# Turning the written key of an RWKV-7 chunk recurrence: PE transposes and ScalarE copies, or a DRAM round trip and VectorE

## The chip, the cores and the metric

The kernel runs on one core of a Trainium2 chip. The metric is device time in microseconds (us) of one execution. The times shown are of three runs; one further execution is profiled.

## What is computed

One layer of a hybrid trunk: batch 1, 512 positions, width 2048, everything in float32. Half of the width is an RWKV-7 group of 16 heads of 64 with a generalized delta rule, the other half a pooling group. In short form:

```
h = rms_norm(x, norm_g);  z = h @ w_in            # columns: r, k, v, two low-rank inputs, gate | pool input, pool gate
zs = zs + (token_shift(zs) - zs) * mu                # r, k, v and the low-rank inputs
w = exp(-exp(-softplus(-(w0 + tanh(wd) @ w_up)) - 0.5));  a = sigmoid(a0 + ad @ a_up)
kk = normalize(k * k_k);  k = k * (1 + (a - 1) * k_a)      # per head of 64
for each t:                                          # 16 heads, state S is 64x64
    S = S * w[t] - (S @ kk[t]) (a[t] * kk[t])^T + v[t] k[t]^T
    y[t] = S @ r[t]
y = head_group_norm(y) + (sum(r * k * r_k)) * v
pool = multiscale means of the pool input - itself, a 256x256 map per group, a scale
x = x + concat(y * silu(gate), pool * silu(pool gate)) @ w_out
x = x + sigmoid(x @ w_pg + b_pg) * (p @ w_ple);  out = rms_norm(x, final_g)
```

## The kernel before

**Work and staging.** The 16 heads are taken as 8 head pairs j of 128 channels, the 512 positions as 8 chunks of 64. A float32 product is split in three matmuls on rounded halves (`mm3`): each weight chunk is loaded as `raw_*` by SP, rounded by ScalarE into `whi_*`, and the rest `wlo_*` is left by VectorE. There are four `raw`, four `whi` and four `wlo` buffers, so a `raw` load waits for the `wlo` that read its buffer last. The names carry the stream and the chunk: `raw_r` chunk 2 belongs to the projection r of the next pair.

**Order.** TensorE (PE) runs in the order in which the program is written (`keep_in_program_order`). Its long projections are a stream of fill matmuls, and `pump(n)` puts n units of that stream between dependent steps of the recurrence. The other engines get their order from a scheduler when the kernel is built; each then runs its list in order. SP issues nearly all DMAs, and stands still while one of them waits.

**One head pair.** `prepare(j)` scales the streams. `bk` (128 channels x 8 chunks x 128) holds the written keys k and the removed keys kk, channels on the partitions. `scores(j)` multiplies `bk` with `ar` into the masked chunk matrices `mt`. Four `nd` DMAs take their 32x32 triangles to DRAM, two `n` DMAs bring them back spread over all partitions. `invert(j)` solves all triangles at once by 31 substitution steps on VectorE (`tm`, then `xw`), stores `xw` as `xd` and loads the inverse `x1`. For pair 0 the steps run without a recurrence beside them; for pair j+1 they are dealt out inside the recurrence of pair j, each after that chunk's leading VectorE instruction (`issue_after`, HS and HN in `step`). `gather(j)` transposes v into `uv` and `bk` into `bkn` (positions on the partitions), lets PE fill, transposes the diagonal block of `x1` on VectorE (`y`), and builds the rest of the inverse with PE (`pq`) and the products `mv`. `norm_key` and `scale_key` (the RECIPROCAL) belong to the pair after.

**Recurrence.** `recur(j)` does per chunk: PE `py` (state times `ar`), VectorE `zs`, PE `pu` (inverse times `zs`), ScalarE copies into `uv`, PE `ps` (`bkn` of the chunk times `uv`), VectorE `sbd`, the next state. The fill between them is HC = 6, 9 and 9 units. Before chunk 1 the scores of pair j+1 are computed (`between`).

Of the kernel before, what the change touches and what calls it, by code (L numbers as in the profile page):

```python
# [9 lines left out]
F32 = mybir.dt.float32  # L10
# [5 lines left out]
P = 128  # L16
T = 512
# [4 lines left out]
NJ = DR // P  # L22
LORA = 64
C = 64
NCH = T // C
# [9 lines left out]
def trunk_kernel(ctx: ExitStack, tc: tile.TileContext, x, p, norm_g, w_in, mu, w0, w_up, a0, a_up,  # L35
                 k_k, k_a, r_k, ln_w, ln_b, w_pool, pool_scale, w_out, w_ple, w_pg, b_pg, final_g, out):
    nc = tc.nc
    PSUM = bass.MemoryType.PSUM
    x, p, w_in, w_out, w_ple, w_pg = x[0], p[0, 0], w_in[0], w_out[0], w_ple[0], w_pg[0]
    out = out[0]  # L40

    cst = ctx.enter_context(tc.tile_pool(name="cst", bufs=1))
    dram = ctx.enter_context(tc.tile_pool(name="dram", bufs=2, space=bass.MemoryType.DRAM))
# [4 lines left out]
    psM = s2.enter_context(tc.tile_pool(name="psM", bufs=3, space=PSUM))  # L48
# [24 lines left out]
    ident = cst.tile([P, P], F32, name="ident")  # L73
# [46 lines left out]
    def dp(o, i):  # L120
        return dprm[:, o + i:o + i + 1]
# [14 lines left out]
    def split(hi, lo, src):  # L136
        c_ = nc.scalar.copy(hi, src)
        nc.vector.tensor_tensor(lo, src, hi.bitcast(F32), ALU.subtract)
        return c_
# [16 lines left out]
    def mm(*a, **k):  # L156
        i = nc.tensor.matmul(*a, **k)  # L157
        return tc.keep_in_program_order(i) if pin[0] else i

    def tr(*a):  # L160
        i = nc.tensor.transpose(*a)
        return tc.keep_in_program_order(i) if pin[0] else i
# [30 lines left out]
    n_ = 0  # L193
# [13 lines left out]
    for kind, nm, j in jobs:  # L207
# [7 lines left out]
        else:  # L215
            g, i = j // 4, j % 2
# [79 lines left out]
    for d in range(KT):  # L296
        xt_half(0, d)
        if d in WPOS:
            c = len(wl_)
# [41 lines left out]
    rw = s2a.enter_context(tc.tile_pool(name="rw", bufs=1))  # L341
# [6 lines left out]
    def load_ab(j):  # L348
        jc = slice(j * P, (j + 1) * P)
        w2 = []  # L350
        for nm, src in (("u", w_up), ("a", a_up)):
            raw = rw.tile([P, P], F32, name=f"{nm}r{j}", tag=f"l{nm}r")
            for h in range(2):
                nc.scalar.dma_start(out=raw[64 * h:64 * h + 64, :], in_=src[0, :, jc])
            w2.append((raw, rw.tile([P, P], F32R, name=f"{nm}s{j}", tag=f"l{nm}s")))
        wab[j] = w2
# [135 lines left out]
    def pump(n):  # L492
        debt[0] += n
        while debt[0] > 0:
            c = next(big, None)
            if c is None:
                debt[0] = 0
                return
            debt[0] -= c
# [9 lines left out]
    def need(nm, j):  # L509
        while (nm, j) not in zt:  # L510
            if next(big, None) is None:
                assert (nm, j) in zt
        return zt[nm, j]
# [36 lines left out]
    st_ = {}  # L550
# [26 lines left out]
    def prepare(j):  # L577
        k_, r_, v_ = need("k", j), need("r", j), need("v", j)
        pw, ipw, tha = pws.pop(j)
        kk = kks.pop(j)  # L580
        if j + 1 < NJ:
            load_ab(j + 1)


        ar = rw.tile([P, NCH // 2, 4, C], F32, name=f"ar{j}", tag="ar", bufs=2)
        bk = rw.tile([P, NCH // 2, 4, C], F32, name=f"bk{j}", tag="bk")
        k4 = kk.rearrange("p (q c t) -> p q c t", c=2, t=C)
        pw4 = pw.rearrange("p (q c) t -> p q c t", c=2)
        i4 = ipw.rearrange("p (q c) t -> p q c t", c=2)
        kp = rw.tile([P, T], F32, name=f"kp{j}", tag="kp")  # L590
        nc.vector.tensor_scalar(kp, tha, dp(33, j), dp(41, j), ALU.mult, ALU.add)
        nc.vector.tensor_tensor(kp, kp, k_, ALU.mult)
        nc.vector.tensor_scalar(tha, tha, 0.5, 0.5, ALU.mult, ALU.add)
        nc.vector.tensor_tensor(ar[:, :, 0::3, :], r_.rearrange("p (q c t) -> p q c t", c=2, t=C),
                                pw4[:, :, :, 1:C + 1], ALU.mult)
        nc.vector.tensor_tensor(bk[:, :, 0::3, :], kp.rearrange("p (q c t) -> p q c t", c=2, t=C), i4, ALU.mult)
        nc.vector.scalar_tensor_tensor(ar[:, :, 1:3, :], k_.rearrange("p (q c t) -> p q c t", c=2, t=C), dp(89, j),
                                       pw4[:, :, :, 0:C], ALU.mult, ALU.mult)
        nc.vector.tensor_tensor(kk, kk, tha, ALU.mult)
        nc.vector.tensor_tensor(bk[:, :, 1:3, :], k4, i4, ALU.mult)  # L600
        nc.vector.scalar_tensor_tensor(kp, r_, dp(49, j), kp, ALU.mult, ALU.mult)
        kph = rw.tile([P, T], F32R, name=f"kph{j}", tag="t", bufs=4)
        kpl = rw.tile([P, T], F32R, name=f"kpl{j}", tag="t", bufs=4)
        split(kph, kpl, kp)

        st_[j] = dict(pw=pw, ar=ar, bk=bk, v_=v_, kp=(kph, kpl))

    def scores(j):
        ar, bk, v_ = (st_[j][n_] for n_ in ("ar", "bk", "v_"))
        kph, kpl = st_[j].pop("kp")  # L610

        mt = rw.tile([P, 2, 8, 2, C], F32, name=f"mt{j}", tag="mt", bufs=2)
        pm = [[psM.tile([P, T], F32, name=f"pm{j}_{par}0", tag="m"),
               psY.tile([P, T], F32, name=f"pm{j}_{par}1", tag="y")] for par in range(2)]
        for par in range(2):
            for q in range(4):
                for h in range(2):
                    rows = slice(64 * h, 64 * h + 64)
                    mm(pm[par][h][:, q * P:(q + 1) * P], bk[rows, q, 2 * par:2 * par + 2, :],
                       ar[rows, q, 2 * par:2 * par + 2, :], start=True, stop=True)  # L620
        for par in range(2):
            for h in range(2):
                nc.vector.tensor_tensor(mt[:, par, h::2, :, :],
                                        pm[par][h].rearrange("p (u a t) -> p u a t", u=4, a=2),
                                        msk[:, par:par + 2, :].unsqueeze(1).to_broadcast([P, 4, 2, C]), ALU.mult)


        ps = psM.tile([P, T], F32, name=f"pbo{j}", tag="m")
        mm(ps, blk, kph, start=True, stop=False)
        mm(ps, blk, kpl, start=False, stop=True)  # L630
        bv = rw.tile([P, T], F32, name=f"bv{j}", tag="bv", bufs=2)
        nc.vector.tensor_tensor(bv, ps, v_, ALU.mult)

        nd = dram.tile([2, 2, 8, 32, 32], F32, name=f"nd{j}", tag="nd")
        for par in range(2):
            pb = 64 * (1 - par)
            for b in range(2):
                rows = slice(pb + 32 * b, pb + 32 * b + 32)
                nc.sync.dma_start(out=nd[par, b].rearrange("u r c -> r u c"),
                                  in_=mt[rows, par, :, 1 - par, 32 * b:32 * b + 32])  # L640
        nb = []
        for i in range(2):
            t_ = rw.tile([P, 16, 32], F32, name=f"n32{j}_{i}", tag=("kk", "kp")[i])
            nc.sync.dma_start(out=t_, in_=nd[:, :, :, 16 * i:16 * i + 16, :].rearrange(
                "a b u r c -> (a b u) r c").unsqueeze(0).to_broadcast([4, 32, 16, 32]))
            nb.append(t_)
        st_[j].update(mt=mt, nb=nb, bv=bv)


    def invert(j):  # L650
# [26 lines left out]

    def gather(j):
        d = st_[j]
        bk, v_, mt = d.pop("bk"), d.pop("v_"), d["mt"]  # L680
        if j + 1 < NJ:
            prepare_key(j + 1)
            decay_and_rate(j + 1)
# [1 line left out]
        uv = rw.tile([P, NCH, P], F32, name=f"uv{j}", tag="uv")  # L685
        ps = psY.tile([P, T], F32, name=f"pv{j}", tag="y")
# [4 lines left out]
        nc.scalar.copy(uv[64:128, 1::2, :], pv[64:128])  # L691


        bkn = rw.tile([P, NCH, P], F32, name=f"bkn{j}", tag="bkn")
        for hf in range(2):
            ps = psM.tile([P, T], F32, name=f"pbk{j}_{hf}", tag="m")
            for i in range(4):
                ch = 4 * hf + i
                tr(ps[:, i * P:(i + 1) * P], bk[:, ch // 2, 2 * (ch % 2):2 * (ch % 2) + 2, :], ident)
            nc.scalar.copy(bkn[:, 4 * hf:4 * hf + 4, :], ps.rearrange("p (c n) -> p c n", n=P))  # L700

        pump(H4)

        d.update(uv=uv, bkn=bkn)
        if j + 1 < NJ:
            norm_key(j + 1)
        pump(H5)
# [4 lines left out]
        x1 = d["x1"]  # L712
# [33 lines left out]
        mv = rw.tile([P, 4, P], F32, name=f"mv{j}", tag="mv")  # L746
# [5 lines left out]

    def recur(j, work, between):
        d = st_.pop(j)
        pw, ar, mt, bv, uv, bkn, mv, x1 = (d[n_] for n_ in ("pw", "ar", "mt", "bv", "uv", "bkn", "mv", "x1"))
        hop = [0]
        HC1, HC2, HC3 = HC
        lead = [None]
# [12 lines left out]
        for ch in range(NCH):  # L771
            par, q = ch % 2, ch // 2
# [7 lines left out]
            if ch > 0:  # L780
# [5 lines left out]
                step()  # L786
                pump(HC1)

            psu = psS.tile([P, T], F32, name=f"pu{j}_{ch}", tag="s")
            mm(psu[:, 0:P], x1[:, 2 * q:2 * q + 2, :], zs, start=True, stop=True)  # L790
            for h in range(2):
# [85 lines left out]
    prepare(0)  # L877
    pump(H3)
    scores(0)
    pump(H2)  # L880
    for _ in invert(0):
        pass
    pump(HT)
    gather(0)
    for j in range(NJ):
        def between():
# [5 lines left out]
        if j + 1 == NJ:  # L892
            pn.append(rw.tile([P, NT, DPLE], F32, name="pn", tag="ar", bufs=2))
            for h in range(2):
                nc.scalar.dma_start(out=pn[0][:, 2 * h:2 * h + 2, :],
                                    in_=p[256 * h:256 * h + 256, :].rearrange("(t p) q -> p t q", p=P))
# [281 lines left out]
```

## Time and profile before

| | |
|---|---|
| time, median of three runs | 1094.34 us (1093.44 to 1331.12) |
| profiled execution, its own time | 1094.06 us |
| span of the profile | 1092.3 us |
| PE busy | 1067.4 us, 98% |
| VectorE (DVE) busy | 707.9 us, 65% |
| ScalarE (ACT) busy | 448.2 us, 41% |
| GpSimd (POOL) busy | 74.4 us, 7% |
| chain that ended last | PE 88%, DVE 5%, DMA 3%, ACT 2% |

A row of the timeline gives the start in us from the beginning of the span, the duration in us, the engine, the line of the kernel, the operation, the tile written and the tiles read, the shape, and in brackets how long the engine stood idle ahead of it and who released it. A row of the waits gives the engine and instruction that waited, what it waited for, and then the sum in us, the times and the longest. A row of a tile gives the count and the shortest, median and longest duration in ns. Between 20 and 1088 us lie the eight pairs and the output projections; the recurrences of pairs 0 to 6 are those with an inversion beside them.

### The profile page before, as it was taken

What the parts mean: (1) busy time and instruction counts of PE and PEld (TensorE: products, weight loads), DVE (VectorE), ACT (ScalarE), POOL (GpSimd) and SP (SyncE); (2) the same over time, 40 slices, a digit from 0 to 9 for tenths busy, and PEclk for the clock granted to TensorE, in tenths of its full rate; (3) what the DMA queues carried; (4) which work ended last, traced back from release to release, by engine and by line L of the source; (5) the groups of instructions that cost most, each with busy time, mean ns of one, the idle gap of its engine ahead of it and who ended that gap; (6) DMA issues with size and microseconds to landing.
All of it is one profiled execution on the core that took longest, in us unless ns stands there. A gap on an engine that the chain in (4) does not pass through costs nothing.

```text
span 1092.3 us, 17194 instructions
## 1 busy us (share of the span) xinstructions
PE 1067.4 (98%) x6060; PEld 879.1 (80%) x6060; DVE 707.9 (65%) x1835; ACT 448.2 (41%) x917; POOL 74.4 (7%) x180
## 2 busy tenths in 40 slices
PE   5999999999999999999999999999999999999996
PEld 4888878888888888787888788888888888888885
DVE  6687867878779679678886956454433424445366
ACT  7633534435335335353443344544222222233337
POOL 2100010110110110100101101000000000000000
PEclk9999999999999999999999999999999999999999
DMA  7433433332423333333334242774534438454534
GB/s 233 116 97 97 112 92 79 102 101 72 127 81 102 105 91 89 95 83 90 94 93 120 79 138 94 231 242 163 171 123 141 164 97 261 129 187 147 174 105 154
DMA packets 178485, 138.56 MB, mean 127 GB/s; under 512 B 34677, under 2 KB 139742, under 8 KB 178398
## 3 DMA queue, kind: packets, MB, share of 16 engines
q1 hardware_dynamic: 157694, 103.89, 32.2%
q10 hardware_dynamic: 20704, 33.56, 9.5%
q8 instruction: 48, 0.79, 0.3%
q14 instruction: 39, 0.32, 0.1%
HBM read 118.02 MB, written 18.87 MB: 125 GB/s over the span
## 4 chain that ended last, share of the span: by engine, by line
PE 88%; DVE 5%; DMA 3%; ACT 2%; issue 1%; SPq 0%; ACTq 0%; DVEq 0%
PE acc_o L157 16%; PE acc_g L157 16%; PE zb L157 15%; PE zv L157 8%; PE zr L157 7%; PE zg L157 7%; PE zk L157 6%; DMA n<-nd 2%; PE py L157 2%; PE pple L157 2%; PE pu L157 2%; PE pm L157 1%; PE pp L157 1%; PE ps L157 1%; PE pmv L157 1%
## 5 line engine op out<-in xcount | busy, mean ns | idle before, releaser
L133 DVE TENSOR_TENSOR wlo_g<-raw_g,whi_g 128x512 fp32r<-128x512 f32 x84 | 56.9, 683 | 78.7 <-ACT whi_g L132 78.5
L157 PE MATMUL zb<-hhi,whi_b 128*128 128x512 f32 x256 | 106.3, 415 | 0.0
L133 DVE TENSOR_TENSOR wlo_o<-raw_o,whi_o 128x512 fp32r<-128x512 f32 x64 | 43.9, 690 | 92.3 <-ACT whi_o L132 92.2
L157 PE MATMUL zb<-hhi,wlo_b 128*128 128x512 f32 x256 | 100.5, 393 | 0.0
L157 PE MATMUL acc_o<-whi_o,ylo 128*128 128x512 f32 x256 | 100.2, 391 | 0.0
L157 PE MATMUL acc_o<-whi_o,yhi 128*128 128x512 f32 x256 | 99.9, 390 | 0.0
L157 PE MATMUL zb<-hlo,whi_b 128*128 128x512 f32 x256 | 99.8, 390 | 0.0
L157 PE MATMUL acc_o<-wlo_o,yhi 128*128 128x512 f32 x256 | 99.7, 389 | 0.0
L132 ACT CAST whi_g<-raw_g 128x512 fp32r<-128x512 f32 x84 | 51.9, 620 | 105.5 <-PE acc_g L157 60.3
L157 PE MATMUL acc_g<-whi_g,x2hi 128*128 128x512 f32 x208 | 81.2, 391 | 0.0
L157 PE MATMUL acc_g<-wlo_g,x2hi 128*128 128x512 f32 x208 | 81.0, 389 | 0.0
L157 PE MATMUL acc_g<-whi_g,x2lo 128*128 128x512 f32 x208 | 80.6, 389 | 0.0
L132 ACT CAST whi_o<-raw_o 128x512 fp32r<-128x512 f32 x64 | 39.9, 623 | 97.8 <-PE acc_o L157 97.8
L813 POOL TENSOR_SCALAR s0p<-sbd,pw 64x64 f32<-64x64 f32 x96 | 56.7, 590 | 338.5 <-DVE sbd L806 253.7
L132 ACT CAST whi_b<-raw_b 128x512 fp32r<-128x512 f32 x64 | 39.7, 620 | 87.1 <-PE zv L157 34.9
L133 DVE TENSOR_TENSOR wlo_b<-raw_b,whi_b 128x512 fp32r<-128x512 f32 x64 | 43.7, 684 | 34.2 <-ACT whi_b L132 33.0
L157 PEld LDWEIGHTS zb<-hhi,wlo_b 128*128 128x128 f32 x256 | 48.0, 188 | 11.0
L661 DVE TENSOR_TENSOR xw<-xw,tm 128x60 f32<-128x60 f32 (+24 forms) x248 | 51.9, 209 | 6.8
L157 PEld LDWEIGHTS acc_o<-wlo_o,yhi 128*128 128x128 f32 x256 | 48.1, 188 | 10.0
L157 PEld LDWEIGHTS acc_o<-whi_o,ylo 128*128 128x128 f32 x256 | 48.1, 188 | 9.9
L157 PEld LDWEIGHTS acc_o<-whi_o,yhi 128*128 128x128 f32 x256 | 48.1, 188 | 9.6
L157 PEld LDWEIGHTS zb<-hhi,whi_b 128*128 128x128 f32 x256 | 48.3, 189 | 8.4
(285 smaller groups left out, 2546.8 us busy)
## 6 DMA issues: line engine op xcount, KB each, us to landing
raw_b<-in_w_in_dram SPq DMA_DIRECT2D x64, 256.0 KB
raw_o<-in_w_out_dram SPq DMA_DIRECT2D x64, 256.0 KB
raw_g<-in_w_pg_dram SPq DMA_DIRECT2D x64, 256.0 KB
raw_k<-in_w_in_dram SPq DMA_DIRECT2D x32, 256.0 KB
raw_r<-in_w_in_dram SPq DMA_DIRECT2D x32, 256.0 KB
raw_v<-in_w_in_dram SPq DMA_DIRECT2D x32, 256.0 KB
raw_g<-in_w_in_dram SPq DMA_DIRECT2D x32, 256.0 KB
n<-nd SPq DMA_DIRECT2D x16, 256.0 KB
```

Source lines behind the costliest of these rows:

```text
L132: nc.scalar.copy(hi, raw)
L133: nc.vector.tensor_tensor(lo, raw, hi.bitcast(F32), ALU.subtract)
L157: i = nc.tensor.matmul(*a, **k)
L661: nc.vector.tensor_tensor(xw[:, 0:n_, s + 1:32], xw[:, 0:n_, s + 1:32], tm[:, 0:n_, 0:w_], ALU.add)
L813: nc.gpsimd.tensor_scalar(s0p[hc, :], nxt[hc, hc], pcn[hc], None, ALU.mult)
```

## The change

`prepare` stores `bk` in DRAM (`bkd`). `scores` reads it back with four DMAs, one per 32 partitions, into `bg` in an order in which each 32x32 block stands where its transpose belongs; `bg` takes the buffer of `bk`. `turn_key(j, half)` transposes 128x512, in 32x32 blocks, from `bg` into `bkn` on VectorE. For pair 0 both halves are turned in `gather(0)`. For pair j+1 the halves are turned in the recurrence of pair j, at chunk 4, when chunks 0 to 3 of the old key have been used, and at chunk 7. There is now one `bkn` for all pairs. The eight PE transposes and two ScalarE copies per pair are gone.

```diff
@@ -603,7 +603,16 @@
         kpl = rw.tile([P, T], F32R, name=f"kpl{j}", tag="t", bufs=4)
         split(kph, kpl, kp)
 
-        st_[j] = dict(pw=pw, ar=ar, bk=bk, v_=v_, kp=(kph, kpl))
+        bkd = dram.tile([P, NCH * P], F32, name=f"bkd{j}", tag="bkd")
+        nc.sync.dma_start(out=bkd, in_=bk.rearrange("p q s c -> p (q s c)"))
+        st_[j] = dict(pw=pw, ar=ar, bk=bk, bkd=bkd, v_=v_, kp=(kph, kpl))
+
+    bkn = rw.tile([P, NCH, P], F32, name="bkn")
+
+    def turn_key(j, hf):
+        cs = slice(4 * hf, 4 * hf + 4)
+        nc.vector.transpose(bkn[:, cs, :].rearrange("p c (b k) -> p (c b) k", k=32),
+                            st_[j]["bg"][:, cs, :, :].rearrange("p c b k -> p (c b) k"))
 
     def scores(j):
         ar, bk, v_ = (st_[j][n_] for n_ in ("ar", "bk", "v_"))
@@ -644,7 +653,11 @@
             nc.sync.dma_start(out=t_, in_=nd[:, :, :, 16 * i:16 * i + 16, :].rearrange(
                 "a b u r c -> (a b u) r c").unsqueeze(0).to_broadcast([4, 32, 16, 32]))
             nb.append(t_)
-        st_[j].update(mt=mt, nb=nb, bv=bv)
+        bg = rw.tile([P, NCH, 4, 32], F32, name=f"bg{j}", tag="bk")
+        for q in range(4):
+            nc.sync.dma_start(out=bg[32 * q:32 * q + 32],
+                              in_=st_[j]["bkd"].rearrange("(b k) (c q i) -> q k c b i", b=4, q=4, i=32)[q])
+        st_[j].update(mt=mt, nb=nb, bv=bv, bg=bg)
 
 
     def invert(j):
@@ -677,7 +690,7 @@
 
     def gather(j):
         d = st_[j]
-        bk, v_, mt = d.pop("bk"), d.pop("v_"), d["mt"]
+        v_, mt = d.pop("v_"), d["mt"]
         if j + 1 < NJ:
             prepare_key(j + 1)
             decay_and_rate(j + 1)
@@ -691,17 +704,12 @@
         nc.scalar.copy(uv[64:128, 1::2, :], pv[64:128])
 
 
-        bkn = rw.tile([P, NCH, P], F32, name=f"bkn{j}", tag="bkn")
-        for hf in range(2):
-            ps = psM.tile([P, T], F32, name=f"pbk{j}_{hf}", tag="m")
-            for i in range(4):
-                ch = 4 * hf + i
-                tr(ps[:, i * P:(i + 1) * P], bk[:, ch // 2, 2 * (ch % 2):2 * (ch % 2) + 2, :], ident)
-            nc.scalar.copy(bkn[:, 4 * hf:4 * hf + 4, :], ps.rearrange("p (c n) -> p c n", n=P))
-
+        if j == 0:
+            turn_key(0, 0)
+            turn_key(0, 1)
         pump(H4)
 
-        d.update(uv=uv, bkn=bkn)
+        d.update(uv=uv)
         if j + 1 < NJ:
             norm_key(j + 1)
         pump(H5)
@@ -752,7 +760,7 @@
 
     def recur(j, work, between):
         d = st_.pop(j)
-        pw, ar, mt, bv, uv, bkn, mv, x1 = (d[n_] for n_ in ("pw", "ar", "mt", "bv", "uv", "bkn", "mv", "x1"))
+        pw, ar, mt, bv, uv, mv, x1 = (d[n_] for n_ in ("pw", "ar", "mt", "bv", "uv", "mv", "x1"))
         hop = [0]
         HC1, HC2, HC3 = HC
         lead = [None]
@@ -786,6 +794,9 @@
                 step()
                 pump(HC1)
 
+            if ch in (4, 7) and j + 1 < NJ:
+                with tc.issue_after(lead[0].ins):
+                    turn_key(j + 1, ch // 7)
             psu = psS.tile([P, T], F32, name=f"pu{j}_{ch}", tag="s")
             mm(psu[:, 0:P], x1[:, 2 * q:2 * q + 2, :], zs, start=True, stop=True)
             for h in range(2):
```

The scheduler also orders other instructions anew. Three places follow. The first is SP, around the scores of pair 3, inside the recurrence of pair 2; `raw_r` and `raw_v` are weight loads for the pair after. Before:

```order
L639 DMA nd_3707<-mt_3677 32x8x32 x4
L129 DMA raw_r_2_2110<-in_w_in_dram 128x4x128
L644 DMA n_0_3712<-nd_3707 128x1x512
L644 DMA n_1_3714<-nd_3707 128x1x512
L129 DMA raw_r_3_2116<-in_w_in_dram 128x4x128
L129 DMA raw_v_0_2153<-in_w_in_dram 128x4x128
```

And now:

```order
L648 DMA nd_3698<-mt_3668 32x8x32 x2
L658 DMA bg_3707<-bkd_3565 32x32x32
L129 DMA raw_r_2_2115<-in_w_in_dram 128x4x128
L648 DMA nd_3698<-mt_3668 32x8x32 x2
L658 DMA bg_3707<-bkd_3565 32x32x32
L129 DMA raw_r_3_2121<-in_w_in_dram 128x4x128
L129 DMA raw_v_0_2158<-in_w_in_dram 128x4x128
L653 DMA n_0_3703<-nd_3698 128x1x512
L653 DMA n_1_3705<-nd_3698 128x1x512
```

Two of the four `bg` loads, and the weight loads `raw_r` 3 and `raw_v` 0, now stand ahead of the two `n` loads.

The second is VectorE at the same place: the first `tm` is the first use of `n`, the `zs` in the first row belongs to chunk 2 and `sbd` is the state after that chunk. Before:

```order
L784 TENSOR_TENSOR zs_568<-py_0_3577,mv_3525 64x128
L657 TENSOR_TENSOR tm_3790<-i_116,n_0_3712 128x31
L661 TENSOR_TENSOR xw_3789<-xw_3789,tm_3790 128x31
L657 TENSOR_TENSOR tm_3790<-xw_3789,n_0_3712 128x30
L661 TENSOR_TENSOR xw_3789<-xw_3789,tm_3790 128x30
L657 TENSOR_TENSOR tm_3790<-xw_3789,n_0_3712 128x29
L133 TENSOR_TENSOR wlo_r_0_2083<-raw_r_0_2080,whi_r_0_2082 128x512
```

And now:

```order
L792 TENSOR_TENSOR zs_568<-py_0_3568,mv_3514 64x128
L133 TENSOR_TENSOR wlo_r_0_2088<-raw_r_0_2085,whi_r_0_2087 128x512
L817 SCALAR_TENSOR_TENSOR sbd_567<-ps_2_3827,pw_2392,s0p_1_3755 64x64
L133 TENSOR_TENSOR wlo_r_1_2094<-raw_r_1_2091,whi_r_1_2093 128x512
L817 SCALAR_TENSOR_TENSOR sbd_567<-ps_2_3827,pw_2392,s0p_1_3755 64x64
L670 TENSOR_TENSOR tm_3786<-i_116,n_0_3703 128x31
L674 TENSOR_TENSOR xw_3785<-xw_3785,tm_3786 128x31
L670 TENSOR_TENSOR tm_3786<-xw_3785,n_0_3703 128x30
L792 TENSOR_TENSOR zs_569<-py_0_3568,mv_3514 64x128
```

The first `tm` has moved from behind `zs` of chunk 2 to behind the `sbd` of that chunk, and three steps of the substitution now stand directly ahead of `zs` of chunk 3 (`zs_569`).

The third is VectorE at the `y` transposes of pair 0, which stand between the inverse and PE's `pq`. Before:

```order
L133 TENSOR_TENSOR wlo_b_1_1051<-raw_b_1_1048,whi_b_1_1050 128x512
L596 TENSOR_TENSOR bk_1648<-kp_1649,ipw_1441 128x4x2x64
L568 TENSOR_SCALAR kk_1421<-pss_1492 128x512
L723 STREAM_TRANSPOSE y_1551<-x_1142 32x256 x2
L572 RECIPROCAL kk_1421<-kk_1421 128x512
L133 TENSOR_TENSOR wlo_b_2_1057<-raw_b_2_1054,whi_b_2_1056 128x512
L133 TENSOR_TENSOR wlo_b_3_1151<-raw_b_3_1148,whi_b_3_1150 128x512
L370 SCALAR_TENSOR_TENSOR sv_1526<-zv_1375,prm,sv_1526 128x511
```

And now:

```order
L133 TENSOR_TENSOR wlo_b_2_1065<-raw_b_2_1062,whi_b_2_1064 128x512
L597 SCALAR_TENSOR_TENSOR ar_1644<-sk_1280,dprm,pw_1448 128x4x128
L601 SCALAR_TENSOR_TENSOR kp_1646<-sr_1380,dprm,kp_1646 128x512
L526 TENSOR_TENSOR as_1643<-ar_1640,as_1643 64x128
L133 TENSOR_TENSOR wlo_b_3_1159<-raw_b_3_1156,whi_b_3_1158 128x512
L370 SCALAR_TENSOR_TENSOR sv_1523<-zv_1383,prm,sv_1523 128x511
L731 STREAM_TRANSPOSE y_1548<-x_1150 32x256
L572 RECIPROCAL kk_1429<-kk_1429 128x512
L731 STREAM_TRANSPOSE y_1548<-x_1150 32x256
```

Work for the next pair (`ar`, `kp`, `as`, `wlo_b`, `sv`) has moved ahead of the first `y`, and the RECIPROCAL between the two.

## The prediction

> **What bounds the kernel now.** I read the page first: the busy shares, the granted clock and the chain that ended last.
>
> ```profile
> span 1092.3 us, 17194 instructions
> PE 1067.4 (98%) x6060; PEld 879.1 (80%) x6060; DVE 707.9 (65%) x1835; ACT 448.2 (41%) x917; POOL 74.4 (7%) x180
> PEclk9999999999999999999999999999999999999999
> PE 88%; DVE 5%; DMA 3%; ACT 2%; issue 1%; SPq 0%; ACTq 0%; DVEq 0%
> ```
>
> PE is busy for 1067.4 of 1092.3 us at a clock that never drops, and 88% of the chain is PE. So whatever leaves PE's program gains its own length, and whatever makes PE stand still costs its own length; the other engines cost nothing until PE waits for them. Next I read what PE waits for in the recurrence.
>
> ```profile
> PE py L157 <- DVE sbd L806: 1.9, 6, 0.6
> PE pu L157 <- DVE zs L784: 0.7, 2, 0.4
> ```
>
> Over 56 chunk steps PE loses 2.6 us to VectorE. The fill matmuls hide the rest, with little to spare, as part 3 shows.
>
> **1. What is removed.** Per head pair, eight PE transposes (`pbk`) and two ScalarE copies.
>
> ```profile
> 111.29 1.04 PE L161 MATMUL pbk<-ident,bk 128*128 128x128 f32 x8
> 112.08 0.48 PE L157 MATMUL zv<-hhi,whi_v 128*128 128x512 f32 x1
> L700 ACT COPY bkn<-pbk x16: 569/590/594, 114.7 to 637.8; 128x512 f32<-128x512 f32 x16
> ```
>
> The next matmul starts 112.08 - 111.29 = 0.79 us after the first transpose. Eight pairs are 6.3 us at least; I take 6.9, since where a later weight load is uncovered the step looks up to 0.3 longer (an estimate). The copies free 16 x 0.59 = 9.4 us of ScalarE, which is busy for 41% and is not on the path: nothing. **Minus 6.9.**
>
> **2. Head pair 0, where nothing covers the inversion.** SP issues nearly every DMA in program order and stands still at each wait. In the new order the loads `raw_r` 3 and `raw_v` 0 stand between `nd` and `n`, and the latter waits for `wlo_r` 0, the VectorE half of the split behind ScalarE's `whi_r`. Before, `n` went out ahead of them.
>
> ```profile
> 82.67 1.22 SPq L644 DMA_DIRECT2D n<-nd  x2
> 86.16 0.62 ACT L132 CAST whi_r<-raw_r 128x512 fp32r<-128x512 f32 x1 [1.60 <-issue]
> 89.14 0.19 DVE L657 TENSOR_TENSOR tm<-i,n 128x31 f32<-128x31 f32 x1 [3.75 <-DMA n<-nd]
> 114.42 0.69 DVE L594 TENSOR_TENSOR ar<-sr,pw 128x512 f32<-128x512 f32 x1
> 115.03 0.69 DVE L133 TENSOR_TENSOR wlo_b<-raw_b,whi_b 128x512 fp32r<-128x512 f32 x1
> 116.83 0.89 DVE L723 STREAM_TRANSPOSE y<-x 32x256 f32<-32x256 f32 x2
> 117.75 3.35 DVE L572 RECIPROCAL kk<-kk 128x512 f32<-128x512 f32 x1
> 122.16 0.74 DVE L370 SCALAR_TENSOR_TENSOR sv<-zv,prm,sv 128x511 f32<-128x511 f32 x1
> 120.59 0.39 PE L157 MATMUL zb<-hhi,wlo_b 128*128 128x512 f32 x1
> 120.90 0.69 PE L157 MATMUL pq<-y,mt 32*32 32x32 f32 x32
> ```
>
> `whi_r` starts at 86.16; 0.62 for it and 0.69 for `wlo_r` give 87.5, and one load ahead about 0.6 more: `n` goes out at 88.1, not 82.67. It took 89.14 - 82.67 = 6.5 us to its first use, so the substitution starts at 94.6: **5.4 late**. From there to the second `y` transpose VectorE is dense, so what the new order puts ahead of `y` adds its own time. That is two turns of 128x512; `ar` second half, `kp`, `as` and `sv`; and the RECIPROCAL, which now stands between the two `y` transposes. A transpose of 32x256 takes 0.89 / 2 = 0.445 us. No row shows 128x512; the bounds are 0.445 for twice the columns and four such in a row, 1.8. I take 0.7, next to the 0.69 of any VectorE pass of that shape: 1.4 for two. The others step every 0.6 (115.03 - 114.42): 0.6 + 0.65 + 0.25 + 0.65 = 2.2, and the RECIPROCAL 3.3. Sum 5.4 + 1.4 + 2.2 + 3.3 = 12.3: `y` ends at 117.7 + 12.3 = 130. PE gets to `pq` at 120.90 - 0.79 = 120.1, with nothing else to do in its fixed order: it stands still for **9.9 us**. The bounds are 5, if RECIPROCAL and `sv` do not come in between in time, and 13, with turns at 1.8 and `n` 1 us slower.
>
> [...]
>
> **3. Head pairs 3 to 7: `n` is late inside the recurrence.** There the `bg` loads stand between `nd` and `n`, and loads that wait for later `wlo` come ahead of `n` too. Pair 3 as the example, in order of the engines:
>
> ```profile
> 289.70 1.15 SPq L644 DMA_DIRECT2D n<-nd  x2
> 293.97 0.62 ACT L132 CAST whi_r<-raw_r 128x512 fp32r<-128x512 f32 x1 [1.96 <-issue]
> 296.34 0.19 DVE L657 TENSOR_TENSOR tm<-i,n 128x31 f32<-128x31 f32 x1 [2.58 <-DMA n<-nd]
> 300.85 0.28 DVE L784 TENSOR_TENSOR zs<-py,mv 64x128 f32<-64x128 f32 x1
> 293.05 0.38 PE L157 MATMUL py<-sbd,ar 128*128 128x128 f32 x2
> 294.65 0.38 PE L157 MATMUL pu<-zs,x 128*128 128x128 f32 x2
> 299.88 0.49 PE L157 MATMUL py<-sbd,ar 128*128 128x128 f32 x2 [0.45 <-DVE sbd L806]
> ```
>
> `n` now waits behind `raw_v` 0, which waits for `wlo_r` 0: 293.97 + 1.3 for the two halves + 0.7 for the issues = 296.0, about 6.3 later than 289.70. At 296.34 - 289.70 = 6.64 to first use, the substitution starts at 302.6 (before: 296.34, while VectorE had nothing urgent). In the new order it stands directly ahead of `zs` of chunk 3. That `zs` was due about 0.4 behind the `py` at 299.88 - 0.45 = 299.43, and `pu` follows `py` by 294.65 - 293.05 = 1.60, so it can be about 0.85 late unnoticed. With the first steps of the substitution ahead of it (0.67 us: three instructions here) `zs` starts at 303.3 and `pu` some 0.5 later, at 303.8; due was 301.03. PE stands still for **2.75 us**, in a recurrence that had 2.6 of such waits in all.
>
> For the other pairs the same formula: stall = (start of the `whi` in question - start of `py` of chunk 2) + 1.15 + what stands between the first `tm` and `zs`. The 1.15 is pair 3's 2.75 - 0.92 - 0.67.
>
> ```profile
> 369.31 0.62 ACT L132 CAST whi_r<-raw_r 128x512 fp32r<-128x512 f32 x1 [2.33 <-PE zk L157]
> 369.34 0.27 PE L157 MATMUL py<-sbd,ar 128*128 128x128 f32 x1
> 443.33 0.62 ACT L132 CAST whi_r<-raw_r 128x512 fp32r<-128x512 f32 x1 [2.59 <-PE zk L157]
> 442.41 0.27 PE L157 MATMUL py<-sbd,ar 128*128 128x128 f32 x1
> 518.50 0.62 ACT L132 CAST whi_r<-raw_r 128x512 fp32r<-128x512 f32 x1 [2.33 <-PE zk L157]
> 518.53 0.27 PE L157 MATMUL py<-sbd,ar 128*128 128x128 f32 x1
> 594.71 0.62 ACT L132 CAST whi_b<-raw_b 128x512 fp32r<-128x512 f32 x1 [1.92 <-PE zb L157]
> 593.83 0.27 PE L157 MATMUL py<-sbd,ar 128*128 128x128 f32 x1
> ```
>
> Pairs 4 and 6: -0.03 + 1.15 + 2.0 (eight steps ahead) = 3.1 each; pair 5: 0.92 + 1.15 + 0.45 = 2.5; pair 7: 0.88 + 1.15 + 0.67 = 2.7. With pair 3's 2.75 the sum is 14.2; the 2.6 of waits that were there go into it: **plus 11.6**. In pair 1 `n` is about 3.6 late, but no `zs` stands close behind, and in pair 2 its place is unchanged: nothing. The bounds are 0, if `n` lands as much earlier as it starts later, and 18, with `n` 1 us slower behind the block loads.
>
> **4. What stands behind the late substitution.** Its 62 small steps per pair must be done by chunk 7, and fewer chunks are left for them, beside up to three weight splits each. VectorE then has up to 7.6 us of work in a chunk whose pitch is 299.43 - 293.05 = 6.4. I take **plus 4** for five pairs, bounds 0 and 8.
>
> **5. What is added and hidden.** The turns at chunks 4 and 7 stand right behind `zs`; 15 fill units lie between `zs` and the `sbd` that needs VectorE next, so 0.7 (or 1.8) is covered. Without that cover 14 turns would cost 10. The store of `bk` and the four `bg` loads are issued by SP, each about 0.5 us, the price of the `n` rows above; that delay of the queue is in parts 2 and 3. How long a `bg` load takes no row shows: it is 1024 runs of 128 bytes. All packets of that ring together give one price.
>
> ```profile
> q1 hardware_dynamic: 157694, 103.89, 32.2%
> DVE tm L657 <- DMA n<-nd: 18.3, 8, 3.8
> ```
>
> 32.2% of 16 x 1092.3 us over 157694 packets is 36 ns each, on packets of 659 bytes on average. 64 of them in a row on each of 16 engines are 2.3 us; 6.6 is the time to first use that `n` took. I take 3.5 to 4, and the order leaves more than that from the last `bg` to its turn, by about 1.4 us in the tightest pair. So nothing, with the upper end as a rival.
>
> **Sum.** Against the profiled execution, 1094.06 us (span 1092.3, and 1.8 around it): 1094.06 - 6.9 + 9.9 + 11.6 + 4 = 1112.7. The median of the runs shown is 1094.34, 0.3 higher: **1113 us**.
>
> **The rivals.**
> - **All of it is hidden (chance 0.12).** `n` lands earlier when it is issued later, since VectorE's wait of 18.3 us in eight pairs shows how long it was alone in coming; then only part 1 counts, 1094.3 - 6.9 = 1087. Against it: `n` of pair 3 is issued 6 us later, and only 0.85 is free at `zs`.
> - **Half of it (0.15).** The stall of pair 0 stays, while in the recurrence `n` starts 2 to 3 us earlier than I work out: each of five stalls falls to about 0.5, and part 4 with it. 1094.3 - 6.9 + 9.9 + 2.5 = 1100.
> - **The blocks come late (0.23), slower than before by more than 2%.** The half key for chunks 0 to 3 is turned in chunk 4, ahead of `sbd` on an engine that works in order. If a `bg` load needs 6.6 us like `n`, the turn waits 1.5 to 2.5 us in each of six or seven pairs, and the same SP queue delivers the weights late. This decides from about 5 us between issue and landing. 6 x 2 = 12 on top of the forecast: 1125. [...]
> - **The chain as forecast (0.50)**, 1104 to 1120 by its own bounds: -6.9 with 6 to 13 in pair 0, 7 to 14 in the recurrence and 2 to 6 behind it, not all at one end.
>
> **How the numbers follow.** The likeliest case gives 1113. The range has to leave out no more than 2 in 10: it starts at 1092, which leaves out the hidden case, and ends at 1128, which leaves out the worst third of the late blocks (2.5 us in seven pairs, and late weights). About 2%, 22 us, is what a measurement of this kernel can tell from no change, so the lines are at 1072.5 and 1116.2. Faster: nothing I can name gets below 1087, 0.02. Slower: the late blocks, 0.22 of their 0.23, and three in ten of the forecast's 0.50, together 0.37. Same: 0.61.
>
> **What would show it.** In the profile after: no `pbk`; PE waits of about 10 us at the first `pq`, with the RECIPROCAL between the two `y` rows; the `n` DMAs of pairs 3 to 7 issued some 6 us later against `py` of chunk 2; `pu` of chunk 3 waiting for `zs` by 2.5 to 3 us in each; the DVE waits of the turn for `bg` near zero. The prediction is wrong if PE does not wait at those places, if the turn waits for `bg`, or if the transposes in 128x512 take several microseconds.

## The result, and the profile after

The changed kernel takes 1122.03 us (median of 6 runs, 1117.58 to 1130.24) against 1094.73: a ratio of 1.0257, with an interval of 1.0214 to 1.0299; the run of 1331.12 us among those of before is not in it. That is slower by 28 us; 1113 had been forecast, with 1092 to 1128 as the range. The profiled execution took 1123.03 us, 29.0 more than the profiled one of before. Its page:

```profile
span 1121.3 us, 17115 instructions
PE 1069.5 (95%) x5996; PEld 877.9 (78%) x5996; DVE 715.7 (64%) x1851; ACT 440.6 (39%) x901; POOL 78.0 (7%) x180
PEclk9999799999999999999999999999999999999999
PE 58%; DVE 5%; DMA 3%; issue 1%; ACT 1%; ACTq 0%; SPq 0%; DVEq 0%
```

PE has 64 transposes fewer, and is yet busy for 2 us longer: in the fifth slice, around 125 us, the granted clock falls to seven tenths, which it did nowhere before. What PE waits for has changed too:

```profile
PE pu L157 <- DVE zs L792: 17.1, 10, 4.1
PE pq L157 <- DVE y L731: 8.8, 2, 5.5
PE pyt L161 <- DVE ysb L862: 1.3, 2, 0.7
PE pm L157 <- DVE bk L600: 1.1, 2, 0.6
PE px L157 <- issue: 0.9, 1, 0.9
PE py L157 <- DVE sbd L817: 0.8, 3, 0.4
```

The first two rows are the two places of the forecast; the next three are new and had not been forecast. Head pair 0 in the timeline of the changed kernel, SP, then VectorE, then PE:

```profile
88.04 0.38 SPq L129 DMA_DIRECT2D raw_v<-in_w_in_dram  x1
88.53 1.21 SPq L653 DMA_DIRECT2D n<-nd  x2
95.28 0.19 DVE L670 TENSOR_TENSOR tm<-i,n 128x31 f32<-128x31 f32 x1 [4.59 <-DMA n<-nd]
125.53 0.43 DVE L731 STREAM_TRANSPOSE y<-x 32x256 f32<-32x256 f32 x1
126.00 3.35 DVE L572 RECIPROCAL kk<-kk 128x512 f32<-128x512 f32 x1
129.26 0.38 DVE L731 STREAM_TRANSPOSE y<-x 32x256 f32<-32x256 f32 x1
126.11 0.28 PE L157 MATMUL pq<-y,mt 32*32 32x32 f32 x2 [5.51 <-DVE y L731]
129.69 1.06 PE L157 MATMUL pq<-y,mt 32*32 32x32 f32 x30 [3.30 <-DVE y L731]
130.68 1.97 PE L157 MATMUL pmv<-uv,mt 64*64 64x64 f32 x32
```

`n` goes out right behind the waiting `raw_v`, at 88.53 (forecast 88.1), and the second `y` is done at 129.64 (forecast 130). PE stands still twice, before and behind the RECIPROCAL, and then `pmv` takes 1.97 us, at half clock; in the kernel before it takes 1.15. Pair 3 on SP and VectorE, and then `pu` of chunk 3 in pairs 3 to 7 on PE:

```profile
306.62 0.39 SPq L129 DMA_DIRECT2D raw_v<-in_w_in_dram  x1
307.12 1.18 SPq L653 DMA_DIRECT2D n<-nd  x2
313.88 0.19 DVE L670 TENSOR_TENSOR tm<-i,n 128x31 f32<-128x31 f32 x1 [3.94 <-DMA n<-nd]
314.55 0.28 DVE L792 TENSOR_TENSOR zs<-py,mv 64x128 f32<-64x128 f32 x1
314.89 0.77 PE L157 MATMUL pu<-zs,x 128*128 128x128 f32 x2 [2.57 <-DVE zs L792]
396.42 0.49 PE L157 MATMUL pu<-zs,x 128*128 128x128 f32 x2 [4.14 <-DVE zs L792]
473.36 0.49 PE L157 MATMUL pu<-zs,x 128*128 128x128 f32 x2 [2.41 <-DVE zs L792]
551.86 0.49 PE L157 MATMUL pu<-zs,x 128*128 128x128 f32 x2 [3.08 <-DVE zs L792]
629.98 0.49 PE L157 MATMUL pu<-zs,x 128*128 128x128 f32 x2 [2.63 <-DVE zs L792]
```

The five waits sum to 14.8 us; 14.2 had been forecast. From the issue of `n` to its first use it takes 313.88 - 307.12 = 6.76 us here, 6.64 before: the transfer is no slower, it starts late. The turns, in the rows of `bkn`:

```profile
L614 DVE STREAM_TRANSPOSE bkn<-bg x16: 696/703/707, 105.7 to 657.5; 128x512 f32<-128x512 f32 x16
```

0.70 us each, as assumed, and no row of VectorE's waits names `bg`: the blocks were always there in time.

Last the granted clock, in windows of 1 us (the columns are the busy times of PE, PEld, DVE, ACT and POOL with their counts, then the clock, the DMA share and GB/s):

```profile
123.00:124.00 1.00, 0.00 (x0) 0.00 (x0) 1.00 (x3) 0.00 (x0) 0.00 (x0) 0.90 0.68 108
136.00:137.00 1.00, 1.00 (x4) 0.81 (x3) 0.18 (x1) 0.00 (x0) 0.00 (x0) 0.50 0.00 0
137.00:138.00 1.00, 1.00 (x5) 0.78 (x5) 0.00 (x0) 0.00 (x0) 0.00 (x0) 0.77 0.37 102
314.00:315.00 1.00, 0.11 (x1) 0.11 (x1) 0.87 (x6) 0.00 (x0) 0.00 (x0) 0.98 0.79 226
318.00:319.00 1.00, 1.00 (x6) 0.82 (x4) 0.70 (x4) 0.15 (x1) 0.00 (x0) 0.82 1.03 259
396.00:397.00 1.00, 0.58 (x3) 0.53 (x4) 0.97 (x4) 0.06 (x1) 0.00 (x0) 0.94 0.15 37
```

Half clock is 0.50, as from 136 to 137. A mean of 0.90 over 1 us is 0.2 us at half clock, so the clock fell at 123.8, and it rose at 137.46; PE was at work again from 129.69. What these 7.8 us at half clock cost shows in the first `pu` of pair 0, before and now:

```profile
126.09 0.38 PE L157 MATMUL pu<-zs,x 128*128 128x128 f32 x2
138.22 0.39 PE L157 MATMUL pu<-zs,x 128*128 128x128 f32 x2
```

From `pq` to that `pu` PE does the same work, but for two of the 32 small `pq`; before it took 126.09 - 120.90 = 5.2 us, now 138.22 - 129.69 = 8.5. That is 3.3 us, and not half of 7.8, as the small matmuls take less than twice as long (`pmv` 1.97 against 1.15). In pair 3 the clock fell at 314.96 and rose at 318.36: half of 3.4, 1.7 us more, as the 128x512 matmuls there start every 0.43 us instead of every 0.23. Pair 4, from 396.88, is like pair 3.

### The profile page after: what moved, and what is told of

Read it like the earlier page. It is cut to its first block, busy times and chain, and to the rows that moved or that the text cites. A ratio compares the mean times of both kernels' runs of the same rounds, so it can differ in the third digit from the quotient of the medians.

```text
span 1121.3 us, 17115 instructions
## 1 busy us (share of the span) xinstructions
PE 1069.5 (95%) x5996; PEld 877.9 (78%) x5996; DVE 715.7 (64%) x1851; ACT 440.6 (39%) x901; POOL 78.0 (7%) x180
## 4 chain that ended last, share of the span: by engine, by line
PE 58%; DVE 5%; DMA 3%; issue 1%; ACT 1%; ACTq 0%; SPq 0%; DVEq 0%
PE acc_o L157 16%; PE acc_g L157 15%; PE zb L157 9%; PE zg L157 4%; PE zv L157 2%; PE zk L157 2%; DMA n<-nd 2%; PE zr L157 2%; PE pple L157 2%; PE py L157 1%; PE pp L157 1%; PE pu L157 1%; DVE tm L670 1%; DVE xw L674 1%; PE pm L157 1%
```

## The experiments

**The order alone.** In the first, the `bg` loads are only kept behind `n`:

```diff
+            with tc.issue_after(nl.ins):          # nl: the second n load
                 nc.sync.dma_start(out=bg[32 * q:32 * q + 32], ...)
```

> The change with one edit: the four bg loads are issued behind both n loads of the same pair. The round trip, the turns and the missing PE transposes stay. Theory of the delayed n: SP's order is again nd, one weight load, n, so the first tm goes back to its old place, the zs waits of pairs 3 to 7 and nearly all of pair 0's wait go, and only the 7 us of PE transposes are left as a difference: 1088, within 1085 to 1092, clock 1.0 throughout. Rival, the turns or the 128-byte block traffic themselves cost the time: still 1105 or more, with turns waiting for bg or VectorE late ahead of sbd.

Measured: 1093.86 us, ratio 0.9988 (0.9977 to 0.9999). The loss of 28 us is gone, with all turns and all block traffic in place. PE's waits in it:

```profile
PE py L157 <- DVE sbd L818: 4.1, 8, 1.2
PE pu L157 <- DVE zs L793: 1.6, 4, 0.6
```

No wait for `y`, and no long wait for `zs`. But 1088 was expected, and 6 us of it did not come; the next three runs look for them.

**The parts one by one.** All three leave the turned key out and multiply `ps` by zeros. Without the trip and without the turns:

```diff
-                mm(pss[:, 0:P], bkn[:, ch, :], uv[:, ch, :], start=True, stop=True)
+                mm(pss[:, 0:P], kz, uv[:, ch, :], start=True, stop=True)
-        nc.sync.dma_start(out=bkd, in_=bk.rearrange("p q s c -> p (q s c)"))
-            nc.sync.dma_start(out=bg[32 * q:32 * q + 32], ...)
-                    turn_key(j + 1, ch // 7)           # and the two of pair 0
```

> The bound of the gain: the change without the round trip and without the turns, so that the turned key is left out (ps multiplies by zeros and the state stays at what that gives); PE's transposes and ScalarE's copies are absent too. SP and VectorE then have the order of before. If the 7.0 us of PE transposes are all gain: 1087.5 (1086 to 1089). Rival, that VectorE sets the end of each pair, so that PE reaches it earlier only to wait: 1090 to 1092, with PE waits at pyt and py in place of the transposes.

Measured: 1092.68 us, ratio 0.9973 (0.9957 to 0.9989). The second theory holds: the PE time saved is 7.5 us (step 1 below), and by the interval only 1 to 5 of it are gained. The rows:

```profile
PE py L157 <- DVE sbd L802: 5.3, 8, 1.8
PE pyt L161 <- DVE ysb L847: 1.3, 2, 0.7
PE pm L157 <- DVE bk L600: 1.1, 2, 0.6
PE px L157 <- issue: 0.9, 1, 0.9
```

The last three, 3.3 us, stand in the changed kernel too, and none of them before. The first two of these are waits at the end of a pair for VectorE: its normalisation of `ysb` and its `bk`. PE, with eight transposes fewer ahead of them, comes too early. For `px` the view names no releaser, and a wait of before, right behind that `px`, is gone in exchange:

```profile
PE pu L157 <- ACT x L745: 1.0, 1, 1.0
```

The waits for `sbd`, 1.9 us before, have grown most. They differ between the versions (4.1 in the first experiment, 2.6 in the next one), and the profiled execution here, 1095.87 us, is one of the slower of its ten.

With the turns and without the trip:

```diff
-        bg = rw.tile([P, NCH, 4, 32], F32, name=f"bg{j}", tag="bk")
-        ...                                            # and both DMAs
+        bg = bk.rearrange("p q (s b) (d k) -> p (q s) (b d) k", s=2, k=32)
```

> As the one before, but with the 16 turns of 128x512 on VectorE, read from bk itself, without the DRAM round trip; again ps multiplies by zeros in place of the turned key. Hidden turns: the same time as without them, within 1 us. Rival, that the 11 us of turns use up VectorE's reserve and are what keeps the change with late bg loads at 1094 instead of 1088: 4 to 6 us more than without them.

Measured: 1091.54 us, ratio 0.9967 (0.9956 to 0.9977), not slower than without turns. 11 us of VectorE work cost nothing that can be measured.

With the trip and without the turns:

```diff
-                    turn_key(j + 1, ch // 7)           # and the two of pair 0; both DMAs stay
```

> As the first of these, but with the DRAM round trip and without the turns: bk is stored and bg loaded as in the change, nobody reads bg, and ps multiplies by zeros in place of the turned key. SP's queue has the order of the change (bg and waiting weight loads ahead of n). Theory of the delayed n: nearly all of the loss is here, 1113 to 1121, with zs waits of 2.5 to 4 us in pairs 3 to 7 and about 9 at pq of pair 0. Rival, that the turns make the loss: below 1100.

Measured: 1122.74 us, ratio 1.0245 (1.0189 to 1.0301), with the waits of the change:

```profile
PE pu L157 <- DVE zs L785: 14.7, 7, 3.1
PE pq L157 <- DVE y L724: 7.5, 2, 4.6
```

So the loss comes with the round trip, though nobody reads what it loads; and the first run shows that it is the place of its loads in the queue, not their traffic. The trip behind `n` against no trip (1093.86 and 1091.54, in different sets of runs) leaves about 2 us for the traffic and the changed order, which was not split further.

**Other queues.** The loads from ScalarE's queue, and from GpSimd's:

```diff
-            nc.sync.dma_start(out=bg[32 * q:32 * q + 32], ...)
+            nc.scalar.dma_start(out=bg[32 * q:32 * q + 32], ...)      # first run
+            nc.gpsimd.dma_start(out=bg[32 * q:32 * q + 32], ...)      # second run
```

> The change with one edit: the four bg loads are issued by ScalarE's queue instead of SP's. Theory of the delayed n: SP never stands still for a bg load, n goes out early, 1088 (1085 to 1095; a ScalarE that stands still for bg's buffer ahead of the uv copies would take it to the upper end). Rival, the turns or the block traffic: 1105 or more, as these are unchanged.

Measured: 1103.4 us, ratio 1.0080 (1.0065 to 1.0095); more than expected. `n` is early, at 83.43 in pair 0, but the scheduler found another order for VectorE, in which the product `sg` stands among the steps of pair 0's substitution instead of ahead of them. The mean granted clock of this run is 0.995, against 0.997 or 0.998 in the runs of before, and PE waits once for `sg`:

```profile
PE zr L157 <- DVE sg L374: 6.3, 1, 6.3
```

> The change with one edit: the four bg loads are issued by GpSimd's queue instead of SP's, so that SP's list is again that of before plus the eight stores. Delayed n as the only cause: 1091 to 1094, like the version with bg behind n, since n goes out early and GpSimd is busy for 7%. If GpSimd's own issue holds up s0p, which stands behind bg in its list and feeds sbd: 1097 to 1105, with PE waits of py for sbd. If the block loads land late from that queue: VectorE waits for bg at the turns.

Measured: 1100.63 us, ratio 1.0053 (1.0032 to 1.0073): the second theory. GpSimd, whose instructions feed `sbd`, waits for the buffer of `bg`, and PE waits for `sbd` longer than in any other version:

```profile
PE py L157 <- DVE sbd L817: 7.1, 8, 2.5
POOL bg L658 <- PE pm L157: 17.8, 5, 4.8
```

**The stall of pair 0, and the clock behind it.** The RECIPROCAL is kept behind both `y`:

```diff
-            with tc.issue_after(yt.ins):
+            with tc.issue_after(ya.ins), tc.issue_after(yt.ins):
                 scale_key(j + 1)
```

> The change with one edit: scale_key, with its RECIPROCAL, has to come behind both y transposes, not only behind the second. In the order of VectorE the RECIPROCAL (3.35) between the two y of pair 0 is exchanged for a kpl subtraction (0.69); all else in the lists is the same but for three rows behind it. Theory: PE's second wait at pq of pair 0 (3.30) falls to about 0.6, with the half clock behind it unchanged: 2.7 less than the change, 1119. Rival, that this wait only hides another (px, or the weights): no change, 1122.

Measured: 1119.44 us, ratio 1.0230 (1.0213 to 1.0247), as expected in size; as the interval overlaps that of the change, the row decides. The wait at `pq` falls by 2.8 us:

```profile
PE pq L157 <- DVE y L730: 6.0, 2, 5.4
```

Then PE is kept at work ahead of `pq` of pair 0 by matmuls whose results are overwritten, 58 in one kernel and 72 in the other:

```diff
+        if j == 0:
+            for _ in range(58):
+                mm(ps3.rearrange("p u c -> p (u c)"), hhi[:, 0, 0:P], hhi[:, 0, 0:256], start=True, stop=True)
```

> The change with 58 additional PE matmuls of 128x256 ahead of pq of pair 0, whose results are overwritten by pq; they fill its idle time by 6 to 9 us and change no other order. Theory of the clock: the stall of pair 0 costs its 8.8 us and then about 3.7 more at half clock; with PE at work in it the clock stays up and 3 to 4 us come back: 1118.5 although PE does more. Rival, the time behind the stall is lost to late weights or VectorE: 1122 or more, and matmuls behind pq still at twice their duration.

Measured: 1126.16 us, ratio 1.0279 (1.0242 to 1.0315): a miss. The profiled execution is the fastest of its four (1119.41 us, the others 1125.84 to 1129.47). It shows that the clock was not kept up, and not what made the others slower:

```profile
119.93 7.11 PE L157 MATMUL pq<-hhi 128*128 128x256 f32 x58
126.97 0.24 PE L157 MATMUL pq<-y,mt 32*32 32x32 f32 x2
128.95 0.88 PE L157 MATMUL pq<-y,mt 32*32 32x32 f32 x30 [1.73 <-DVE y L731]
129.76 1.97 PE L157 MATMUL pmv<-uv,mt 64*64 64x64 f32 x32
```

1.73 us of waiting and a few 32x32 matmuls were left, and the clock fell behind them, at 129.24, and rose at 136.06: `pmv` again takes 1.97. So 14 more were added:

> The change with 72 additional PE matmuls instead of 58 ahead of pq of pair 0, which leaves less than 0.3 us idle there. With 58 the clock still fell, 2.2 us after the last of them, in 1.7 us of waiting and small 32x32 matmuls. If idle time is what lowers the clock, it now stays at 1.0 from 120 to 140 us and pu of chunk 0 comes about 3 us earlier than with 58. If the small matmuls alone do it, or the matmuls added, it falls again.

The `pmv` row of this kernel, and the window from 126 to 137 us:

```profile
130.14 1.15 PE L157 MATMUL pmv<-uv,mt 64*64 64x64 f32 x32
126.00:137.00 11.00, 10.24 (x141) 8.96 (x140) 7.38 (x8) 3.85 (x10) 0.40 (x1) 1.00 0.33 108
```

The clock stays up here (1.00) and `pmv` takes 1.15; from `pq` to the first `pu` it is 134.74 - 129.53 = 5.2 us again. This one execution took 1114.97 us. That is close to the 1113 of the forecast's chain, which has no term for the clock, but in part by luck: the mean granted clock is 0.995, against 0.998 in the profiled execution of before, and 0.003 of 1113 us is an estimated loss of 3 us that the chain did not have. The same kernel, timed:

> The same kernel as the one with 72 additional matmuls, timed. If the half clock behind pair 0 is worth 3 to 4 us and the rest of the spread comes from the clock behind the stalls of pairs 3 to 7: median 1115 to 1119, below that of the change. If the one look at it was luck: 1122 like the change.

Measured: 1118.34 us, ratio 1.0218 (1.0201 to 1.0234), 0.0039 below that of the change: about 4 us, for the 3.3 of the rows. The two intervals overlap, so it is the `pmv` rows and the clock that show the cause, and the times only agree with it. In the four runs the mean granted clock is 0.992, 0.994, 0.995 and 0.997: the same kernel, and not the same time at half clock.

**A version that beats both.** The `bg` loads behind `n`, and four fill units moved to where PE now comes too early:

```diff
-    H1, H2, H3, H4, H5, HE = 6, 12, 20, 8, 13, 40
+    H1, H2, H3, H4, H5, HE = 6, 12, 20, 8, 17, 40
-    HC, HT, HX = (6, 9, 9), 130, 13
+    HC, HT, HX = (6, 9, 9), 130, 9
```

> The version with bg behind n, with four fill units moved from behind the PE transposes of ysb (pyt) to ahead of them (H5 17 instead of 13, HX 9 instead of 13). If PE's new waits at the end of a pair (1.3 us at pyt, 0.9 at px) are what eats the PE time saved: 1092.5, 1 to 1.5 us less than without the move. If px or pq then wait for what is no longer covered: the same or more.

Measured: 1090.46 us, ratio 0.9959 (0.9946 to 0.9973). The waits at `pyt` and `px` are gone; that at `pm` has grown, from 1.1 to 2.9 us:

```profile
PE pm L157 <- DVE bk L600: 2.9, 2, 1.5
```

The control is the kernel before with the same two lines:

> A control for the version with the four fill units moved: the kernel before (PE transposes, no round trip) with the same move, H5 17 and HX 9. If the move only takes the PE waits that the missing transposes uncovered, it gains nothing here: 1094 to 1095.5. If it is an improvement of its own, as large as there: 1091 to 1092, and the turned key adds nothing to it.

Measured: 1095.09 us, ratio 1.0005 (0.9993 to 1.0017). The move gains nothing there; it only brings back what the missing transposes had uncovered.

## Why the prediction was right, and where it was not

The direction and the chain were right, and the time lies in the range; but 1113 was 9 us short, and "within 2%" was the likeliest outcome where it came out just beyond. Slower than that had 0.37, more than half of it for the late blocks, which did not happen. By its steps:

- **1, the transposes.** -6.9 was nearly the right length and the wrong gain. The same PE instructions stand 0.87 us earlier behind six of the eight removed groups, 1.1 and 1.2 behind the other two, 7.5 us in all. But 3.3 us come back as waits at `pyt`, `pm` and `px`, for 1.0 at `pu` that went. The step asked what hides the transposes' cost and not who PE meets earlier without them. The rival in which everything else is hidden, 1087, is therefore not to be had with this fill: the version with neither trip nor turns takes 1092.7.
- **2, pair 0.** 9.9 forecast, 8.8 measured: PE came to `pq` 0.5 later than worked out, at 120.6, went on 0.3 earlier, at 129.69, and worked for 0.3 in between. The RECIPROCAL's share is shown by taking it out, 2.8 us. In the first experiment the wait at `pq` is gone altogether, but there `n` and the RECIPROCAL are both back in their old places, so the share of `n` by itself was not measured.
- **2, the clock.** The sum has no term for it, and the kernel before does not show it: its granted clock is 1.00 from 20 to 700 us. This is the part that failed: 3.3 us in pair 0, and 1.7 each in pairs 3 and 4, 6.7 together, of 9 missing. The trace shows the clock at 0.50 for 13.66 us in pair 0, 7.8 of them with PE at work, and for 3.40 each in pairs 3 and 4; in pair 3 that was behind a stall of only 2.57 us.
- **3, `n` inside the recurrence.** 14.2 forecast, 14.8 measured: pair by pair 2.75, 3.1, 2.5, 3.1 and 2.7 against 2.57, 4.14, 2.41, 3.08 and 2.63. Pair 4 is 1 us over: there `n` took 7.8 us to its first use, not 6.64, as it had before the change too. That the order is the cause is shown by the first experiment, and that the turns and the loads' traffic are not by the others.
- **4, what is displaced.** +4 forecast; 2.3 us of `zs` waits beyond those five are there (17.1 - 14.8), and `sbd` waits fell by 1.1. Smaller than put; the waits of step 1, which the sum lacked, made up for it, by luck.
- **5, the turns and the blocks.** Nothing, as forecast. The late blocks, the rival for the slower side, did not happen: no turn waited for `bg`. How long a load takes is still shown by no row, but it has a bound now: in pair 1, the tightest, the last load was issued at 166.69 and the turn ran at 172.50 without a wait, so it took at most 5.8 us.

The sum by measured terms: -7.5 + 8.8 + 14.8 + 2.3 - 0.7 - 1.1 - 1.0 (waits of before for `zs`, `sbd` and `x` that went) + 3.3 + 6.7 = 25.6, of 29.0 between the two profiled executions. 0.5 of the rest is already there at 20 us, in the start. Another 1.1 comes from how a wait is counted: only from the end of the matmul ahead, which takes 0.39 us, where the next one would have started after 0.23. By the starts of the same PE instructions in both traces the stall of pair 0 costs 9.1 and the five of `zs` 15.7. The last 1.8 is not accounted for.

Of the spread of the changed kernel, 1117.58 to 1130.24 where before runs stay within 1093 to 1095 but for one, the mean granted clock tells most: the fastest run has 0.992, the slowest 0.982. The difference, 0.010 of some 1120 us, is at most 11 us, as half clock while PE stands still costs nothing. It does not tell all: two runs with 0.989 took 1118.83 and 1123.03, and the four with 72 added matmuls, at 0.992 to 0.997, lie within 1 us. That the clock fell behind a stall of 2.57 us and stayed up behind one of 3.08 in the same trace fits such a spread, and the kernels without long stalls (clock 0.996 to 0.998) spread less: by 4 us in the first experiment, by 7 without trip and turns.

## What to carry to other kernels

A DMA added to a queue that works in order is priced by what it lets ahead of the next urgent one, not by its bytes: list the queue before and after, and look for loads that wait between a store and its read-back. Where PE is the bound and work leaves it, check what PE then reaches early: without moving the fill, half of the gain or more came back as waits. And here half clock came on top of some PE stalls: 3.3 us behind the 8.8 of pair 0 and 1.7 each behind the 2.57 of pair 3 and the 4.14 of pair 4, but nothing behind the 2.41 to 3.08 of pairs 5 to 7. So give the clock a term in the sum.

## What the runs showed of the hardware

Between 30 and 700 us the granted clock of the changed kernel stood at 1.00 or at 0.50. It was down from 123.8 to 137.46 us, for 13.66, from 314.96 to 318.36 and from 396.88 to 400.28, for 3.40 each. In the kernel with the RECIPROCAL behind both `y` it was down from 123.28 to 133.52, for 10.24, and with 58 added matmuls from 129.24 to 136.06, for 6.82. The windows from which these ends are worked out, as above: the rise in pair 4 of the changed kernel, then fall and rise in the other two.

```profile
400.00:401.00 1.00, 1.00 (x14) 0.81 (x14) 0.47 (x2) 0.00 (x0) 0.00 (x0) 0.86 0.06 8
123.00:124.00 1.00, 0.00 (x0) 0.00 (x0) 1.00 (x3) 0.62 (x1) 0.00 (x0) 0.64 0.37 75
133.00:134.00 1.00, 1.00 (x5) 0.82 (x4) 0.96 (x2) 0.00 (x0) 0.00 (x0) 0.74 0.01 4
129.00:130.00 1.00, 1.00 (x34) 0.94 (x36) 1.00 (x2) 0.09 (x1) 0.00 (x0) 0.62 0.00 0
136.00:137.00 1.00, 1.00 (x6) 0.83 (x5) 0.00 (x0) 0.00 (x0) 0.00 (x0) 0.97 0.31 76
```

The length of a stall alone does not say whether the clock falls. In the changed kernel it fell within the 5.51 us of pair 0 and behind the 2.57 of pair 3 and the 4.14 of pair 4, and stayed at 1.00 around the 2.41, 3.08 and 2.63 of pairs 5, 6 and 7:

```profile
465.00:480.00 15.00, 12.59 (x72) 10.11 (x71) 8.91 (x41) 4.32 (x11) 2.56 (x4) 1.00 0.49 118
545.00:560.00 15.00, 11.92 (x70) 9.57 (x70) 10.45 (x46) 4.11 (x10) 1.80 (x4) 1.00 0.40 103
622.00:640.00 18.00, 15.25 (x86) 12.09 (x85) 11.52 (x45) 4.75 (x12) 3.07 (x4) 1.00 0.40 102
```

With 58 added matmuls it fell behind a stall of 1.73 us, and with 72 it stayed at 1.00 behind one of 0.76. What decides was not shown.

The way back took different times. From PE's first matmul behind the stall to the rise it was 3.47 us in pair 3 of the changed kernel (314.89 to 318.36), 3.86 in pair 4 (396.42 to 400.28) and 7.77 in pair 0 (129.69 to 137.46). In pairs 3 and 4 PE ran 128x128 matmuls in that time; in pair 0 it ran 32x32 and 64x64 ones until 133.58, and 128x128 ones from there. With 58 added matmuls PE was likewise at work for all of the 6.82 us, on the small ones until 132.65. No run tried this by itself.
